# One step of a hybrid decoder on one core: first weights split a quarter ahead, S5 begun two steps later

## The chip, the core and the metric

The kernel runs on one core of one Trainium2 chip. Its five engines work through queues of their own, in order: PE multiplies matrices, DVE (VectorE) and ACT (ScalarE) do elementwise work, POOL (GpSimd) does a little of it and issues most of the transfers between memory and the core's own buffers, SP issues the loads of the weights. An instruction that waits holds up everything behind it on its engine. The metric is the device time of one execution in microseconds (us).

## The reference

One layer serves 1024 tokens of a prompt and 8 single sample tokens together, 1032 columns in all, with a model width of 2048. All arithmetic is float32.

```
h = rmsnorm(x, g_pre);  proj = h @ w_in            # 2048 -> 10240
q, k, v, za, ub, zb, ga, gb = split(proj)
ya = (retention(q, k, v) * silu(za)) @ w_pa        # 8 heads of 128, chunks of 128
yb = (s5(ub) * silu(zb)) @ w_pb                    # diagonal state space, 64 groups of 16 inputs, 64 states
merged = sigmoid(ga) * ya + sigmoid(gb) * yb
out = x + rmsnorm(merged @ w_out, g_post)
```

The final retention and S5 states are outputs too. The S5 branch builds per group a small Toeplitz matrix from its decay parameters, multiplies it with the inputs ub and carries the state from chunk to chunk.

## The kernel before, in words

**Products.** Each float32 operand is split in a high part `hi` (a cast on ACT) and a low part `lo` (what the cast dropped, a subtraction on DVE), and a product is hi·hi + hi·lo + lo·hi, three matmuls. A weight tile ("quarter") is 128 output rows by 512 inputs: `wtile` loads it on SP into `wraw`, casts it to `whi`, subtracts into `wlo`. There are three buffers of each, a, b and c, used in turn. PE cannot use a quarter's low part before DVE has subtracted it.

**The start.** Input rows are loaded and split while the first two blocks of `ub` (128 rows each) are multiplied. Then `linear` multiplies blocks 2 and 3 of `ub` (`M_UB + 2`, `M_UB + 3`, four quarters each, named (34,0) to (35,3) below: 34 and 35 are their numbers among the blocks of `w_in`). Beside these two blocks the *forms* of the input are built (`build_forms`): sums and differences of input blocks, made on DVE into tiles `fo` and `fx` and written by ACT's queue to the memory tensor `fm_d`. Then come two blocks of v, (16,·) and (17,·). The work beside a product is kept in the queue `bg` of generators; `slot()` advances the first of them by one piece, at the points where the main program calls it.

`wnext` gives `linear` its next quarter. If the list `todo` names quarters, it prepares one more than it hands out, so that the next quarter's split is written ahead of the current quarter's products. If `todo` is empty, it prepares a quarter at the moment of its use.

**The steps.** The rest of the multiplication goes by Strassen-like steps. A step `s` is one pair of output blocks for one half of the input; it has seven products, n = 0 to 6, of 24 pairs of matmuls each (L950), and DVE or ACT takes each result out of PE's accumulators (`evac_st`) into tiles `p1`, `u2`, `u3` and `st`, two buffers of each. Four results of a step are finished blocks. At the first visit of a pair they are written to `pt_d`; at the second visit `result` adds what lies in `pt_d` to the tile with an accumulating transfer (L1024) and, four products later, writes a `v` tile out to `v_d` (L1031). All of these go through POOL's queue.

The first six pairs (two of ub, three of v, one of za) are visited in steps 0 to 5, the "short pass", and again in steps 6 to 11, where they are finished. `B0` is 6. From step 12 on, every pair is at a first visit again, until `C0` = 43, where the second pass begins with forms that are staged from step 41 (`change`, with its first twelve loads on SP).

**S5** runs as generators beside the steps: `s5_params` (small DVE operations on parameters) begins at step `B0 + 1`, `s5_all` at `B0 + 4`. For each of 16 blocks, `s5_mats` loads `bc` (L616) and then fills part of the memory tensor `t_d` with zeros: a memset of the tile `zz` on POOL (L619) and a transfer of it, 128 x 4 rows of 112 numbers (L620). There is one `zz` buffer, at a place in the tile `a15` that the ub rows used before, so the memset of one block waits until the transfer of the block before has landed. `zz` shows as `a` in the profile. DVE's first operation on a block reads `bc` (L624).

**What sets the order.** A scheduler places the instructions of each engine. It keeps data dependencies and waits, but it may place an instruction without open dependencies ahead of where the program wrote it. So the 16 zero-fills, which depend only on each other and on `a15`, do not stand one to a block on POOL's queue: they follow each other from the moment on which `a15` is free.

Of the kernel before, what the change touches and what calls it, by code (L numbers as in the profile page):

```python
# [79 lines left out]
def emit(ctx, tc, I, O):  # L80
# [91 lines left out]
    def slot():  # L172
        with ExitStack() as after:
            for ins in anchor.values():
                after.enter_context(tc.issue_after(ins))
            while bg:
                try:
                    next(bg[0])
                    return
                except StopIteration:  # L180
                    bg.popleft()

    def drain():
        while bg:
            slot()
# [6 lines left out]
    def wquarter(wd, m, kq):  # L192
        return wtile(wd[m, :, 4 * kq:4 * kq + 4, :])
# [17 lines left out]
    def wtile(src):  # L211
        turn[0] += 1
        n = turn[0] % (3 + len(more))
        if "pool" in raw_of:
            raw = raw_of["pool"].tile([128, 4, 128], F32, name="wr")
        else:
            raw = more[n] if n < len(more) else wp.tile([128, 4, 128], F32, name="wraw")
        anchor["s"] = nc.sync.dma_start(raw if len(src.shape) == 3 else raw.rearrange("p a b -> p (a b)"), src).ins
        hi, lo = wpair()
        anchor["a"] = A.copy(hi, raw).ins  # L220
        anchor["v"] = sub(lo, raw, hi.bitcast(F32)).ins
        return hi, lo

    def three(ps, w, i, x, t0, t1, first, last):
        wh, wl = w
        xh, xl = x
        T.matmul(ps, wh[:, i, :], xh[:, t0:t1], start=first, stop=False)
        T.matmul(ps, wh[:, i, :], xl[:, t0:t1], start=False, stop=False)
        anchor["p"] = T.matmul(ps, wl[:, i, :], xh[:, t0:t1], start=False, stop=last).ins
# [10 lines left out]
    todo, ahead = deque(), {}  # L240
# [14 lines left out]
    def linear(wd, m, kt, x, evac, thirds=(0, 1, 2), tick=None):  # L255
        ps = {}
        nq = kt // 4
        for kq in range(nq):
            w = wnext(wd, m, kq)
            for t in thirds:  # L260
                t0, t1 = THIRDS[t]
                if kq == 0:
                    ps[t] = mmbank()
                for i in range(4):
                    k = 4 * kq + i
                    three(ps[t][:, 0:t1 - t0], w, i, x(k), t0, t1, k == 0, k == kt - 1)
                if kq == nq - 1:
                    evac(t, ps[t][:, 0:t1 - t0])
                if tick is not None:
                    tick(kq, t)  # L270
            slot()
# [53 lines left out]
    def x_of(k):  # L325
        return xs[k][:, 0, :], xs[k][:, 1, :]
# [15 lines left out]
    def evac_ub(j):  # L342
        def f(t, ps):
            u = ub_new(j) if t == 0 else ubp[j]
            t0, t1 = THIRDS[t]
            w = min(t1, SEQ) - t0
            mul(perm(u, t0 // 8, w // 8), cs(ps[:, 0:w]), cs(rstd[:, t0:t0 + w]))
            if t == 2:
                mul(u[:, 0, 0:8], ps[:, w:w + 8], rstd[:, SEQ:TOK])
                mul(u[:, 7, 136:144], ps[:, w:w + 8], rstd[:, SEQ:TOK])  # L350
                P.dma_start(ub_d[j * 128:(j + 1) * 128], u)
        return f
# [17 lines left out]
    w_in = I["w_in"]  # L370
    M_UB, M_ZB, M_GA, M_GB = 32, 40, 48, 64
# [7 lines left out]
    with tc.tile_pool(name="start", bufs=3) as sp:  # L379
        banks = [[mmbank() for _ in range(3)], [mmbank(), mmbank(), misc()]]  # L380
        w = None
        sqs = deque()
        for k in range(KD):
# [3 lines left out]
            for n, (a, b) in enumerate(parts):  # L387
                nc.sync.dma_start(xr[:, a:b], I["xT"][k, :, a:b])
                if k % 4 == 0 and n == 0:
                    w = [wquarter(w_in, M_UB, k // 4)]  # L390
# [55 lines left out]
    def first_rms():  # L446
        yield
        yield from rms_bcast(ssq, rstd, rm, 1)
# [3 lines left out]
    next(forms_a)  # L452
    bg.append(first_rms())
    bg.append(forms_a)
    for j in (2, 3):
        linear(w_in, M_UB + j, KD, x_of, evac_ub(j), tick=lambda kq, t: slot())

# [351 lines left out]
    def s5_out():  # L809
        A.dma_start(O["s5p"], s5p["fin"])  # L810
        yield
# [4 lines left out]
    def evac_v(h):  # L816
        def f(t, ps):
            t0, t1 = THIRDS[t]
            s = st_tile()[:, 0:t1 - t0]
            mul(s, ps, rstd[:, t0:t1])  # L820
            A.dma_start(v_d[h, :, t0:t1], s)
        return f
# [5 lines left out]
    def popen(name, side, bufs):  # L828
        st = ExitStack()
        return st, st.enter_context(tc.tile_pool(name=name, bufs=bufs, side=side))  # L830
# [10 lines left out]
    B0, C0, N2 = NA, NA + NP, 2 * NP  # L841
# [70 lines left out]
    def prep(g):  # L912
        s, n = divmod(g, 7)
        if g >= lim[0]:
            return
        r = raws

        def sm(name, a, b):
            r[s, name] = wp.tile([128, 4, 128], F32, name="wraw")
            add(r[s, name], r[s, a], r[s, b])  # L920

        if n == 1:
            sm("s1", "21", "22")
            sm("s2", "s1", "11")
        elif n == 3:
            sm("s3", "11", "21")
        elif n == 6:
            sm("s4", "12", "s2")
        f = r[s, ("11", "s2", "12", "s3", "s1", "22", "s4")[n]]
        hi, lo = wpair(qtile_of(steps[s][0], n, 0))  # L930
        anchor["a"] = A.copy(hi, f).ins  # L931
        anchor["v"] = sub(lo, f, hi.bitcast(F32)).ins
        wforms[g] = hi, lo
# [344 lines left out]
    for part_ in range(2):  # L1278
        for j in range(2):
            for kq in (2 * part_, 2 * part_ + 1):  # L1280
                w = wquarter(w_in, 16 + j, kq)
                if part_ and j and kq == 3:
                    prep(0)
                for t, (t0, t1) in enumerate(THIRDS[0:3]):
                    for i in range(4):
                        k = 4 * kq + i
                        three(ps2[j][t][:, 0:t1 - t0], w, i, x_of(k), t0, t1, k == 0, k == KD - 1)
                    if kq == 3:
                        evac_v(j)(t, ps2[j][t][:, 0:t1 - t0])
                slot()  # L1290
# [57 lines left out]
    def stg_open(bufs):  # L1348
        opened["n"] = bufs
        opened["stg"], opened["stgp"] = popen("stg3", "left", bufs)  # L1350
# [43 lines left out]
    for s in range(N2):  # L1394
        kh, p = steps[s]
        if s == 1:
            drain()
            gstack.close()
            fstack, fb2 = popen("fb2", "left", 1)
            bg.append(build_forms(1, fb2, 4, 4, 2))  # L1400
        if s == B0 - 2:
            drain()
            fstack.close()
            gstack, stg = popen("stg1", "left", 12)
        if s == B0 + 1:
            drain()
            gstack.close()
            qstack, s5q = popen("s5q", "left", 1)
            tstack, s5t = popen("s5t", "left", 1)
            bg.append(s5_params())  # L1410
        if s == B0 + 4:
            drain()
            tstack.close()
            tstack, s5w = popen("s5w", "left", 1)
            bg.append(s5_all())
            bg.append(s5_out())
        if s == C0 - 2:
            drain()
            tstack.close()
            qstack.close()  # L1420
            gstack, stg = popen("stg2", "left", 12)
        if s == C0 + 1:
            gstack.close()
            kstack, k2p["pool"] = popen("k2p", "left", 1)
            k2p["bufs"] = 6
            bg.append(order_y())
            cur["cs"] = act.tile([128, 2, TOK], F32, name="a12")
            A.dma_start(cur["cs"][:, 0], I["cos"])
            A.dma_start(cur["cs"][:, 1], I["sin"])
        if s == C0 + 12:  # L1430
            drain()
            kstack.close()
            rstack, rp = popen("ret", "left", 1)
            bg.append(retention())
            kstack, k2p["pool"] = popen("k2q", "left", 1)
            k2p["bufs"] = 3
        if s == N2 - 2:
            while "done" not in K:
                slot()
            rstack.close()  # L1440
            stg_open(8)
        if s == N2 - 1:
            drain()
            kstack.close()
            zstack, zzp = popen("zz", "right", 4)
        for n in range(7):
            g = 7 * s + n
            if n == 1:
                fetch(s + 1)
            prep(g + 2)  # L1450
            evac_st(g, product(g))
            change(g, B0 - 2, 0)
            change(g, C0 - 2, 1)
            transition(g, N2 - 2, "glu", nc.sync)
            late_work(g)
            if s == C0 + 16 and n == 5:
                kstack.close()
                kstack, k2p["oo"] = popen("oo", "right", 1)
            slot()
# [461 lines left out]
```

## Time and profile before

| what | value |
|---|---|
| median of 3 runs | 2549.42 us (2543.85 to 2551.03) |
| the profiled execution | 2547.51 us, span of its instructions 2545.7 us |
| PE busy | 2502.6 us, 98% of the span |
| DVE busy | 2011.6 us, 79% |
| ACT, POOL busy | 997.5 us, 783.0 us |
| chain that ended last | PE 75%, DVE 5%, issue 4%, DMA 2% |

A timeline row gives an instruction's start and duration in us, engine, line, what it writes and reads, and in brackets how long its engine stood idle before it and what ended that. Line L85 is a helper through which all two-operand DVE operations go, so there the tile names tell what is done. A windows row gives the busy time of each engine in a stretch, then the granted PE clock as a share of full speed, the busy share of the DMA engines and what they moved. PE is busy nearly always; what a change can win or lose shows in the few places where PE stands idle or runs at a lower clock.

### The profile page before, as it was taken

To read this page: it belongs to the slowest core of one execution; us is meant where nothing else is said; L and a number is where in the kernel's file an instruction comes from. 1 tells how busy PE (TensorE), PEld (TensorE's weight loads), DVE (VectorE), ACT (ScalarE), POOL (GpSimd) and SP (SyncE) were. 2 spreads that over 40 slices of the span, in tenths; PEclk is the share of its full clock that TensorE was granted. 3 is DMA by queue.
4 is the path that set the end of the run, shared out by engine and by line. 5 is a ranking of instruction groups with operands and counts; after the bars stand their busy time and mean duration, and the time that the engine had idled before them with its cause. 6 is when DMAs were issued, how large, how long until landed. Compare 5 with 4: busy or idle time off the path is not lost.

```text
span 2545.7 us, 52887 instructions
## 1 busy us (share of the span) xinstructions
PE 2502.6 (98%) x20026; PEld 2454.4 (96%) x20026; DVE 2011.6 (79%) x4212; ACT 997.5 (39%) x1787; POOL 783.0 (31%) x1308
## 2 busy tenths in 40 slices
PE   9899999999999999999999999999999999999998
PEld 8899999999999999999999999999999999999976
DVE  7567897988988987667986676667897788989885
ACT  7042532333333332353334434444552432445532
POOL 0021235222223222123335444443332222433320
PEclk9999999999999999999999999999999999999999
DMA  7769666444344344488889988887888689857784
GB/s 243 237 212 307 191 172 194 128 136 132 121 133 131 125 131 158 154 224 210 213 218 262 240 222 221 216 231 223 290 280 291 213 244 311 297 198 176 210 302 140
DMA packets 238559, 530.77 MB, mean 208 GB/s; under 512 B 34928, under 2 KB 62016, under 8 KB 237536
## 3 DMA queue, kind: packets, MB, share of 16 engines
q0 software_dynamic: 106080, 310.20, 42.8%
q1 hardware_dynamic: 93280, 162.47, 20.3%
q10 hardware_dynamic: 38944, 54.71, 6.7%
q8 instruction: 158, 2.59, 0.4%
q14 instruction: 97, 0.79, 0.1%
HBM read 351.88 MB, written 175.37 MB: 207 GB/s over the span
## 4 chain that ended last, share of the span: by engine, by line
PE 75%; DVE 5%; issue 4%; DMA 2%; POOL 1%; ACT 0%; DVEq 0%; POOLq 0%; ACTq 0%
PE acc L950 65%; PE acc L1819 5%; DVE u L85 1%; DVE a L85 1%; PE misc L780 1%; PE misc L779 1%; PE misc L1175 1%; PE misc L1185 1%; PE misc L1154 1%; PE misc L730 1%; DMA t_d<-a 0%; PE misc L1187 0%; DVE wlob L85 0%; DMA a<-mg_d 0%; DMA stg<-fo_d 0%
## 5 line engine op out<-in xcount | busy, mean ns | idle before, releaser
L950 PE MATMUL acc<-a,whib 128*128 128x256 f32 (+1 forms) x3816 | 631.2, 284 | 7.0 <-DVE u L85 5.9
L950 PE MATMUL acc<-a,whic 128*128 128x256 f32 (+1 forms) x3808 | 629.9, 284 | 7.1 <-DVE u L85 5.6
L950 PE MATMUL acc<-a,whia 128*128 128x256 f32 (+1 forms) x3800 | 627.1, 284 | 0.8 <-ACT whia L931 0.5
L950 PEld LDWEIGHTS acc<-a,whib 128*128 128x128 f32 x3816 | 527.5, 189 | 9.8 <-DVE u L85 5.4
L950 PEld LDWEIGHTS acc<-a,whic 128*128 128x128 f32 x3808 | 525.9, 188 | 10.4 <-DVE u L85 3.5
L950 PEld LDWEIGHTS acc<-a,whia 128*128 128x128 f32 x3800 | 523.6, 188 | 5.6 <-issue 3.0
L950 PE MATMUL acc<-a,wlob 128*128 128x256 f32 (+1 forms) x1908 | 397.5, 283 | 0.0
L950 PE MATMUL acc<-a,wloc 128*128 128x256 f32 (+1 forms) x1904 | 396.9, 283 | 0.4 <-DVE wloc L85 0.4
L950 PE MATMUL acc<-a,wloa 128*128 128x256 f32 (+1 forms) x1900 | 395.1, 282 | 0.0
L950 PEld LDWEIGHTS acc<-a,wloc 128*128 128x128 f32 x1904 | 298.2, 188 | 1.4 <-DVE wloc L85 1.4
L950 PEld LDWEIGHTS acc<-a,wlob 128*128 128x128 f32 x1908 | 298.9, 188 | 0.3
L950 PEld LDWEIGHTS acc<-a,wloa 128*128 128x128 f32 x1900 | 297.0, 188 | 0.3 <-DVE wloa L85 0.2
L931 ACT CAST whic<-wraw 128x512 fp32r<-128x512 f32 x148 | 92.0, 622 | 239.6 <-PE acc L950 178.5
L931 ACT CAST whia<-wraw 128x512 fp32r<-128x512 f32 x146 | 90.7, 621 | 230.2 <-PE acc L950 163.3
L931 ACT CAST whib<-wraw 128x512 fp32r<-128x512 f32 x146 | 90.8, 622 | 230.0 <-PE acc L950 166.4
L85 DVE TENSOR_TENSOR wraw<-wr 128x512 f32<-128x512 f32 x220 | 151.0, 687 | 2.9 <-DVE mhalf L1101 0.4
L85 DVE TENSOR_TENSOR wloa<-wraw,whia 128x512 fp32r<-128x512 f32 x154 | 105.6, 686 | 55.1 <-ACT whia L931 37.3
L85 DVE TENSOR_TENSOR wloc<-wraw,whic 128x512 fp32r<-128x512 f32 x156 | 107.0, 686 | 50.8 <-ACT whic L931 36.7
L931 ACT CAST whib<-wr 128x512 fp32r<-128x512 f32 x111 | 68.9, 621 | 196.3 <-PE acc L950 161.7
L85 DVE TENSOR_TENSOR a<-stg,a 128x516 fp32r<-128x516 f32 (+1 forms) x224 | 136.1, 639 | 10.2 <-ACT a L274 5.7
L931 ACT CAST whia<-wr 128x512 fp32r<-128x512 f32 x110 | 68.3, 621 | 190.6 <-PE acc L950 168.7
L931 ACT CAST whic<-wr 128x512 fp32r<-128x512 f32 x109 | 67.7, 621 | 186.1 <-PE acc L950 154.3
(458 smaller groups left out, 4255.1 us busy)
## 6 DMA issues: line engine op xcount, KB each, us to landing
wr<-in_w_in SPq DMA_DIRECT2D x296, 256.0 KB
pt_d<-u POOLq DMA_DIRECT2D x74, 258.0 KB, 3.3
u<-pt_d POOLq DMA_DIRECT2D x74, 258.0 KB, 5.0
wr<-in_w_out SPq DMA_DIRECT2D x64, 256.0 KB
wr<-in_w_outB SPq DMA_DIRECT2D x64, 256.0 KB
stg<-fm_d POOLq DMA_DIRECT2D x60, 258.0 KB, 4.7
pt_d<-st POOLq DMA_DIRECT2D x37, 258.0 KB, 3.7
pt_d<-p POOLq DMA_DIRECT2D x37, 258.0 KB, 3.0
```

Source lines behind the costliest of these rows:

```text
L85: return (eng or V).tensor_tensor(out, a, b, op)
L730: T.matmul(ps[:, q * 144:(q + 1) * 144], W1[:, g, :], U[:, g, :], start=True, stop=True)
L779: T.matmul(o, Tm[:, g, :], U[:, g, 0:136], start=True, stop=False)
L780: T.matmul(o, W3[:, g, 1:9, :], X[:, g, 0:136], start=False, stop=True)
L931: anchor["a"] = A.copy(hi, f).ins
L950: anchor["p"] = T.matmul(o, a[:, i, :], x, start=first and i == 0 and a is wh and b is xh, stop=n in (2, 5, 6) and i == 3 and a is wl, ski ...
L1154: T.matmul(ps[:, c * 128:(c + 1) * 128], kt[:, 4 * i + c, :], vt[:, 4 * i + c, :], start=True, stop=True)
L1175: T.matmul(ps[:, c * 128:(c + 1) * 128], kT[:, cs], qT[:, cs], start=True, stop=True)
L1185: T.matmul(o, S[:, n], vt[:, n], start=True, stop=n == 0)
L1819: anchor["p"] = T.matmul(ps[c], a, b, start=k == 0 and a is xh and b is wh, stop=k == KD - 1 and a is xl).ins
```

## The change

Two edits, both of order; nothing is computed differently.

```diff
     bg.append(first_rms())
     bg.append(forms_a)
+    todo.extend((w_in, m, kq) for m in (M_UB + 2, M_UB + 3) for kq in range(4))
+    todo.append((w_in, 16, 0))
     for j in (2, 3):
         linear(w_in, M_UB + j, KD, x_of, evac_ub(j), tick=lambda kq, t: slot())
...
-                w = wquarter(w_in, 16 + j, kq)
+                w = ahead.pop((16 + j, kq), None) or wquarter(w_in, 16 + j, kq)
...
         if s == B0 + 1:
             drain()
             gstack.close()
+        if s == B0 + 3:
             qstack, s5q = popen("s5q", "left", 1)
             tstack, s5t = popen("s5t", "left", 1)
             bg.append(s5_params())
-        if s == B0 + 4:
+        if s == B0 + 6:
             drain()
             tstack.close()
             tstack, s5w = popen("s5w", "left", 1)
```

The first edit names the eight quarters of ub blocks 2 and 3, and the first quarter of v, in `todo`, so that each is split one quarter ahead. The second moves the start of `s5_params` from step 7 to step 9, and that of `s5_all` from step 10 to step 12. Lines from 455 on stand two lower in the changed file, from 1408 on three lower.

**DVE, blocks 2 and 3 of ub, where the forms are made.** Before: `wloc_952` is the low part of quarter (35,1), `wloa_1011` that of (35,2), `wlob_1053` that of (35,3); `fx_624` and `fx_626` are the third pair of input blocks whose forms are made.

```order
L428 SCALAR_TENSOR_TENSOR fx_626<-fx_626,g_pre_107,rstd_104 128x1032
L85 TENSOR_TENSOR fo_934<-fx_624 128x516
L85 TENSOR_TENSOR fo_936<-fx_624,fx_626 128x516
L85 TENSOR_TENSOR fo_938<-fx_626,fo_934 128x516
L85 TENSOR_TENSOR wloc_952<-wraw_949,whic_951 128x512
L85 TENSOR_TENSOR fo_940<-fx_626,fo_938 128x516
L428 SCALAR_TENSOR_TENSOR fx_898<-fx_898,g_pre_107,rstd_104 128x1032
L428 SCALAR_TENSOR_TENSOR fx_900<-fx_900,g_pre_107,rstd_104 128x1032
L85 TENSOR_TENSOR fo_993<-fx_898 128x516
L85 TENSOR_TENSOR fo_995<-fx_898,fx_900 128x516
L85 TENSOR_TENSOR fo_997<-fx_900,fo_993 128x516
L85 TENSOR_TENSOR wloa_1011<-wraw_1008,whia_1010 128x512
```

In the changed kernel `wloc_888` is the low part of (35,1) and `wloa_958` that of (35,2):

```order
L85 TENSOR_TENSOR fo_872<-fx_620,fx_622 128x516
L85 TENSOR_TENSOR fo_874<-fx_622,fo_870 128x516
L85 TENSOR_TENSOR wloc_888<-wraw_885,whic_887 128x512
L85 TENSOR_TENSOR fo_876<-fx_622,fo_874 128x516
L85 TENSOR_TENSOR ubp_604<-ubp_604,rstd_104 128x128x8
L85 TENSOR_TENSOR ubp_604<-ubp_604,rstd_104 128x8 x2
L428 SCALAR_TENSOR_TENSOR fx_624<-fx_624,g_pre_107,rstd_104 128x1032
L428 SCALAR_TENSOR_TENSOR fx_626<-fx_626,g_pre_107,rstd_104 128x1032
L85 TENSOR_TENSOR fo_940<-fx_624 128x516
L85 TENSOR_TENSOR fo_942<-fx_624,fx_626 128x516
L85 TENSOR_TENSOR fo_944<-fx_626,fo_940 128x516
L85 TENSOR_TENSOR wloa_958<-wraw_955,whia_957 128x512
```

Each low part moved forward by one group of forms: (35,1) stands ahead of the third pair's forms, at the place behind the second pair's third `fo`; (35,2) stands where (35,1) stood; and the low part of (35,3) takes the place behind the fourth pair's third `fo`, where (35,2) stood.

**POOL, from the last write of ub rows on (step 9).** Before, two zero-fills (`a15`) stand ahead of the load of `bc` for S5's first block:

```order
L1009 DMA ub_d_84<-a14_3784 128x1152
L619 MEMSET a15_4470 128x112
L1031 DMA v_d_88<-st_4249 128x516
L620 DMA t_d_85<-a15_4470 128x4x112
L1024 DMA u3_4294<-pt_d_101 128x516
L619 MEMSET a15_4470 128x112
L620 DMA t_d_85<-a15_4470 128x4x112
L616 DMA bc_4468<-in_bc 128x256
L1024 DMA p1_4150<-pt_d_101 128x516
```

In the changed kernel the zero-fills begin at the same place, behind the same write of ub rows, but the load of `bc` has moved back by two steps; these are its neighbours (`u3_4766` and `st_4723` are results of step 11):

```order
L621 MEMSET a15_4938 128x112
L622 DMA t_d_85<-a15_4938 128x4x112
L1026 DMA st_4723<-pt_d_101 128x516
L621 MEMSET a15_4938 128x112
L622 DMA t_d_85<-a15_4938 128x4x112
L1033 DMA v_d_88<-st_4723 128x516
L621 MEMSET a15_4938 128x112
L622 DMA t_d_85<-a15_4938 128x4x112
L1026 DMA u3_4766<-pt_d_101 128x516
L618 DMA bc_4936<-in_bc 128x256
```

Between the write of ub rows and `bc` stand thirteen zero-fills now, where two stood, and among them all accumulating transfers and stores of steps 9 and 10 and two of step 11.

**DVE, where it first reads `bc`.** Before, in the order of its queue:

```order
L85 TENSOR_TENSOR u2_4202<-acc_4318,u2_4202 128x516
L85 TENSOR_TENSOR wlob_4438<-wr_4169,whib_4437 128x512
L624 TENSOR_SCALAR a15_4470<-bc_4468,sgn_3499 128x64
L85 TENSOR_TENSOR B1_4474<-cr_3743,bc_4468 128x64
L85 TENSOR_TENSOR a15_4470<-ci_3744,a15_4470 128x64
```

And in the changed kernel:

```order
L85 TENSOR_TENSOR u2_4681<-acc_4786,u2_4681 128x516
L85 TENSOR_TENSOR wloa_4906<-wr_4648,whia_4905 128x512
L626 TENSOR_SCALAR a15_4938<-bc_4936,sgn_3989 128x64
L85 TENSOR_TENSOR B1_4942<-cr_4241,bc_4936 128x64
L85 TENSOR_TENSOR a15_4938<-ci_4242,a15_4938 128x64
```

The neighbours are the same (`u2` is the last result of a step), two steps later: step 9's `u2` before, step 11's now.

## The prediction

> **What bounds the kernel now.** I began with the page. PE is busy for all but 43 us of the span, so an edit of order can win or lose only where PE stands still.
>
> ```profile
> span 2545.7 us, 52887 instructions
> PE 2502.6 (98%) x20026; PEld 2454.4 (96%) x20026; DVE 2011.6 (79%) x4212; ACT 997.5 (39%) x1787; POOL 783.0 (31%) x1308
> ```
>
> The list of PE's waits names the places. The largest is one wait for a low part of a weight; the next, summed over nine waits, is for results that DVE takes out of PE's accumulators.
>
> ```profile
> PE acc L950 <- DVE u L85: 11.7, 9, 3.6
> PE mm L229 <- DVE wloc L85: 9.2, 1, 9.2
> ```
>
> *The first place* is quarter (35,1). Its high part was cast long before. On DVE the subtraction stands behind forms that wait until earlier forms have been written to memory:
>
> ```profile
> 85.06 1.97 DVE L85 TENSOR_TENSOR ubp<-ubp,rstd 128x1024 f32<-128x1024 f32 x1
> ...
> 93.53 1.30 DVE L85 TENSOR_TENSOR fo<-fx 128x516 f32<-128x516 f32 x2 [3.34 <-DMA fm_d<-fo]
> ...
> 95.36 0.69 DVE L85 TENSOR_TENSOR wloc<-wraw,whic 128x512 fp32r<-128x512 f32 x1
> ...
> 104.42 0.68 DVE L85 TENSOR_TENSOR wloa<-wraw,whia 128x512 fp32r<-128x512 f32 x1
> ```
>
> The casts of (35,1), (35,2) and (35,3), in that order, show that ACT is not what is late:
>
> ```profile
> 74.64 0.62 ACT L220 CAST whic<-wraw 128x512 fp32r<-128x512 f32 x1 [7.26 <-PE mm L228]
> 80.52 0.62 ACT L220 CAST whia<-wraw 128x512 fp32r<-128x512 f32 x1 [5.26 <-DVE ubp L85]
> 86.54 0.62 ACT L220 CAST whib<-wraw 128x512 fp32r<-128x512 f32 x1 [5.40 <-PE mm L229]
> ```
>
> On PE, these rows are the start of (35,1), its wait, the wait of (35,2), the start of (35,3) and that of the quarter after it; the windows row shows the clock after the wait.
>
> ```profile
> 85.82 0.34 PE L227 MATMUL mm<-a,whic 128*128 128x384 f32 x1
> ...
> 96.10 0.69 PE L229 MATMUL mm<-a,wloc 128*128 128x384 f32 x1 [9.17 <-DVE wloc L85]
> ...
> 105.16 0.44 PE L229 MATMUL mm<-a,wloa 128*128 128x384 f32 x1 [1.35 <-DVE wloa L85]
> ...
> 110.56 0.34 PE L227 MATMUL mm<-a,whib 128*128 128x384 f32 x1
> ...
> 116.21 0.34 PE L227 MATMUL mm<-a,whic 128*128 128x384 f32 x1
> ```
>
> ```profile
> 96.00:100.00 4.00, 3.90 (x12) 3.90 (x13) 3.15 (x4) 0.00 (x0) 0.00 (x0) 0.50 1.03 406
> ```
>
> An undisturbed quarter takes 116.21 - 110.56 = 5.65 us. Three took 116.21 - 85.82 = 30.4 instead of 16.95, so 13.4 us were lost: 9.17 and 1.35 of waiting, and the rest, 2.9, while PE ran at half its clock after the wait.
>
> *The second place* is the start of S5. PE stalls twice on an evacuation (the first and third row); the others are the starts of following products.
>
> ```profile
> 374.96 1.23 PE L950 MATMUL acc<-a,whic 128*128 128x256 f32 x4 [3.28 <-DVE u L85]
> ...
> 379.20 0.64 PE L950 MATMUL acc<-a,whia 128*128 128x256 f32 x4
> ```
>
> ```profile
> 422.08 1.16 PE L950 MATMUL acc<-a,whib 128*128 128x256 f32 x4 [3.60 <-DVE u L85]
> ...
> 426.58 0.64 PE L950 MATMUL acc<-a,whic 128*128 128x256 f32 x4
> ...
> 429.40 0.64 PE L950 MATMUL acc<-a,whia 128*128 128x256 f32 x4
> ```
>
> A product takes 429.40 - 426.58 = 2.82 us, a step of seven 19.7. The products behind the stalls took 4.24 and 4.50, so 1.4 and 1.7 more. The two stalls cost 3.28 + 1.4 = 4.7 and 3.60 + 1.7 = 5.3 us, together 10.0. What is behind them stands in DVE's rows:
>
> ```profile
> 364.02 0.68 DVE L85 TENSOR_TENSOR wlob<-wr,whib 128x512 fp32r<-128x512 f32 x1
> 369.20 0.32 DVE L624 TENSOR_SCALAR a<-bc,sgn 128x64 f32<-128x64 f32 x1 [4.50 <-DMA bc<-in_bc]
> ...
> 374.22 0.68 DVE L85 TENSOR_TENSOR u<-p,acc 128x516 f32<-128x516 f32 x1
> ...
> 412.87 1.10 DVE L85 TENSOR_TENSOR ksb<-AR,B 128x512 f32<-128x512 f32 x1 [5.68 <-DMA t_d<-ksb]
> ```
>
> Both times DVE waits for a transfer that POOL issued late, `bc` and then the store of `ksb`, and the evacuation stands behind. POOL's rows tell why it is late:
>
> ```profile
> 365.10 0.19 POOL L619 MEMSET a<- 128x112 f32 x1 [1.43 <-DMA t_d<-a]
> 365.61 0.78 POOL L620 DMA_DIRECT2D t_d<-a  x1 [0.31 <-POOL a L619]
> 366.37 0.56 POOL L616 DMA_DIRECT2D bc<-in_bc  x1
> 366.90 0.95 POOL L1024 DMA_DIRECT2D p<-pt_d  x1
> ...
> 379.27 0.20 POOL L619 MEMSET a<- 128x112 f32 x1 [1.91 <-DMA t_d<-a]
> 379.77 0.75 POOL L620 DMA_DIRECT2D t_d<-a  x1 [0.30 <-POOL a L619]
> ...
> 382.30 0.19 POOL L619 MEMSET a<- 128x112 f32 x1 [0.26 <-DMA t_d<-a]
> ...
> 387.71 0.19 POOL L619 MEMSET a<- 128x112 f32 x1 [1.99 <-DMA t_d<-a]
> ...
> 405.95 0.19 POOL L619 MEMSET a<- 128x112 f32 x1 [2.71 <-DMA t_d<-a]
> ```
>
> Each memset of a zero-fill waits for the transfer before it, and the accumulating loads and stores of the v blocks queue up behind.
>
> **The first edit, term by term.** It adds no instruction; it moves four subtractions of 0.69 us on DVE, and loads on SP. The low part of (35,1) now stands where DVE was at 85.06, so it is ready by 85.8, and (35,1) runs from 85.8 to 91.5 without a wait. (35,2) does 0.7 us of high-part matmuls and waits from 92.2 for its low part, which has the old place of (35,1) and ends at 95.36 + 0.69 = 96.05. The 1.97 us of ub scaling that now follow the moved split push nothing: DVE stood idle for 3.34 us at 93.53. So PE waits 3.9 us, pays 1.4 for the clock as at 374.96, and ends (35,2) at 96.05 + 4.95 + 1.4 = 102.4. (35,3) works 0.35 us, waits for the place of the row at 104.42, until 105.1, and ends at 105.1 + 5.3 = 110.4. That is 5.8 us before 116.21. Two of the moved weight loads, 256 KB each, now fall among the writes that the forms wait for; at the 406 GB/s of the window each takes 0.65 us there, and part of that falls on the path. I take a gain of **5.0**. Bounds: 0, if forms and low parts get later by as much as they moved, and 13.4, if no wait were left. A loss is not among them, since DVE's idle time covers 0.69 us per split. Behind the place PE runs nearly without a stop until step 9, so the gain stays; DVE's forms keep their end, as they wait for transfers.
>
> **The second edit, term by term.** It adds and removes no instruction either. `s5_params`, all of S5's DVE, ACT and PE work, and POOL's loads of `bc`, U, X, `x0` and the `ksb` stores move back two steps, 39.4 us. Not so the zero-fills: on POOL they begin behind the same write of ub rows as before. So POOL has eleven more of them ahead of `bc`. With P for the time from one zero-fill's memset to the next, `bc` is issued 11 P + 0.95 us after its place of before (0.95 for one accumulating load more, the row at 366.90), while DVE comes to it 39.4 us later. The lateness grows by 11 P + 0.95 - 39.4.
>
> For P the trace has: 3.03 us, the shortest (379.27 to 382.30); 4.56, the mean of four between 387.71 and 405.95, with v traffic among them as it will be; 5.1, the mean of the eight from 365.10 to 405.95, which have S5's own loads among them too; and 3.9 from the median landing of 3.4 plus 0.5 from memset to issue.
>
> ```profile
> t_d<-a POOLq DMA_DIRECT2D x13, 224.0 KB, 3.4
> ```
>
> In the changed kernel S5's loads are gone from between, so I take 4.4, just under the nearest row. Then `bc` is later by 48.4 + 0.95 - 39.4 = 10.0 us, DVE's wait grows from 4.5 to 14.5, and PE's stall at the fourth product of step 12 from 3.28 to 13.3. Behind DVE's waiting instruction stand the rest of that block's first operations, a split, a weight sum and the evacuation `u`, the same as now (369.20 to 374.22). With 2.9 for the clock, as after the wait of 9.17, the new stall costs **16.2**. It takes the place of the old first one (4.7). The old second one (5.3) goes: by the time DVE reaches the next `ksb`, POOL has had the stall to work off its queue, and only three zero-fills are left. The edit costs 16.2 - 10.0 = 6.2.
>
> The end of S5 comes two steps nearer to the staging of the second pass. SP's loads for it could start here, and ACT first read them here:
>
> ```profile
> 1007.77 0.80 SPq L889 DMA_DIRECT2D stg<-fm_d  x2
> ```
>
> ```profile
> 1061.73 0.63 ACT L274 CAST a<-stg 128x516 fp32r<-128x516 f32 x1
> ```
>
> Moved by 39.4, the loads start at 1047.2, 14.5 us ahead of that read. I cost this at nothing; without that cover each further microsecond would be one of PE's, and SP's weight loads stand behind these transfers.
>
> **The sum.** -5.0 + 6.2 = +1.2 us: 2547.51 + 1.2 = 2548.7 for the profiled execution. The median of the runs is 1.9 above that execution, so I forecast **2550 us**: no change, which here means within 0.3% (7.6 us), about what a measurement of this kernel can tell.
>
> **Rivals.**
>
> *Short zero-fills: faster.* If P is near the shortest row, 3.03, then 11 P + 0.95 = 34.3 is less than 39.4, `bc` is in time, and both old stalls go: -10.0 - 5.0 = -15.0, 2534 us. The change is faster than 0.3% as soon as the new stall costs less than 7.4 in all, which is P below about 3.75. For it: with `bc`, U, X and `ksb` gone from between, POOL's queue and the transfers are freer. Against it: the four periods in the stretch most like the coming one average 4.56. The Trainium skill, page "DMA: Bandwidth & Descriptors", section "Anatomy of one DMA — SWDGE (gpsimd) path", fits a transfer from this queue as about 2.0 us plus its bytes over 436 GB/s; for 224 KB that is an estimate of 2.5 us, so P near 3.0 and this rival's time. The trace agrees in its shortest case (379.77 to 382.30, 2.53 us) and not in its median of 3.4.
>
> *Long zero-fills: slower.* At P = 5.1 the lateness grows by 17.7, the stall is 20.9 + 2.9 = 23.8, and the whole is +8.8, 2558 us. It decides from P = 5.0 on. For it: that was the mean over the eight periods, and accumulating loads and stores of three steps now crowd between zero-fills without a pause. Against it: those eight held loads of S5 that have left. The Trainium skill, same page, section "Specifications", wants pieces of at least 512 bytes for full rate; a zero-fill's rows are 448 bytes. No row here separates that from waiting in the queue.
>
> *The first edit gives nothing,* because the writes of forms bound the stretch (DMA share 1.03 in the window) and PE only waits elsewhere: +6.2, 2555.6, still no change.
>
> *The change does not move the stall at all,* since the zero-fills, which make POOL late, are not moved: then DVE waits about as before, -5.0, 2544, no change.
>
> **How the numbers follow.** Forecast 0.42, first edit void 0.07, stall as before 0.06: same 0.55. Short zero-fills 0.28: faster. Long ones 0.17: slower. The range runs from the rival at 2534 to just past the one at 2558: 2534 to 2560. The likeliest case alone, with P from 3.9 to 4.8, spans 2544 to 2556.
>
> **What would show it.** Right: PE has no wait of 9 us near 86, but two of 2 to 4 near 92 and 103, and the v quarters start about 5 us earlier; DVE's wait for `bc` near step 12 is 10 us or more, with one PE stall of as much; thirteen memsets lie between the last ub write and `bc` on POOL; no `ksb` wait of DVE afterwards. Wrong: `bc` in time, or a PE stall on stage loads near 1060. The forecast falls if P is outside 3.75 to 5.0.

## The result, and the profile after

| | median | range | runs |
|---|---|---|---|
| kernel before | 2549.72 us | 2543.85 to 2554.17 | 20 |
| changed kernel | 2546.10 us | 2541.58 to 2550.60 | 20 |

The ratio is 0.9985, with a 95% interval of 0.9978 to 0.9992: 3.6 us faster by the medians, 2.0 to 5.6 by the interval. That is inside the 0.3% which I called no change, and inside my range of 2534 to 2560. But with twenty runs each it is clear of nothing, and it goes the other way than the +1.2 that I had forecast. The sum came out about 5 us too high.

The profiled execution of the changed kernel took 2549.9 us, near the upper end of its runs, and that of before (2547.51) lies in the lower half of its own. So these two profiles stand +2.4 apart where the medians stand -3.6 apart. They are compared place by place below, never by their spans.

```profile
span 2548.1 us, 52901 instructions
PE 2503.8 (98%) x20026; PEld 2456.2 (96%) x20026; DVE 2010.5 (79%) x4212; ACT 996.7 (39%) x1787; POOL 781.2 (31%) x1308
```

The list of PE's waits (total, number, longest) still has the same two kinds on top, but the longest of each is now at a new place:

```profile
PE acc L952 <- DVE u L85: 15.9, 8, 10.6
PE mm L229 <- DVE wloa L85: 8.1, 1, 8.1
```

*The first place*, in the timeline of the changed kernel (DVE's and PE's rows; start, duration, instruction, idle time before it):

```profile
87.24 0.34 PE L227 MATMUL mm<-a,whic 128*128 128x384 f32 x1
...
96.91 0.70 DVE L85 TENSOR_TENSOR fo<-fx 128x516 f32<-128x516 f32 x1 [4.00 <-DMA fm_d<-fo]
...
101.11 0.68 DVE L85 TENSOR_TENSOR wloa<-wraw,whia 128x512 fp32r<-128x512 f32 x1
...
101.85 0.69 PE L229 MATMUL mm<-a,wloa 128*128 128x384 f32 x1 [8.10 <-DVE wloa L85]
...
114.30 0.34 PE L227 MATMUL mm<-a,whic 128*128 128x384 f32 x1
```

Quarter (35,1) no longer waits. (35,2) waits 8.1 us for a low part that I had expected ready at 96.05 and that was ready at 101.8; (35,3) then does not wait at all. The three quarters took 114.30 - 87.24 = 27.06, that is 10.1 more than three undisturbed ones (16.95); before it was 13.4. In this pair of profiles the first edit gained 3.3 us at its place.

*The second place* is the start of S5. POOL's, DVE's and PE's rows:

```profile
352.39 0.19 POOL L621 MEMSET a<- 128x112 f32 x1 [0.48 <-DMA ub_d<-a]
358.88 0.19 POOL L621 MEMSET a<- 128x112 f32 x1
...
406.46 0.19 POOL L621 MEMSET a<- 128x112 f32 x1
408.26 0.92 POOL L618 DMA_DIRECT2D bc<-in_bc  x1
...
413.23 0.26 DVE L626 TENSOR_SCALAR a<-bc,sgn 128x64 f32<-128x64 f32 x1 [11.90 <-DMA bc<-in_bc]
...
418.88 1.23 PE L952 MATMUL acc<-a,whib 128*128 128x256 f32 x4 [10.62 <-DVE u L85]
...
423.76 0.64 PE L952 MATMUL acc<-a,whic 128*128 128x256 f32 x4
```

The mechanism is the forecast one: thirteen memsets stand ahead of `bc`, DVE waits for `bc`, PE for the evacuation behind it. The sizes are smaller: P is (406.46 - 358.88) / 11 = 4.33 (4.4 forecast), DVE's wait 11.9 (14.5), PE's stall 10.6 (13.3). The product behind the stall took 423.76 - 418.88 = 4.88 instead of 2.82, so 2.1 for the clock (2.9). The windows rows show it (PE clock is the column before the last two):

```profile
416.00:420.00 4.00, 1.12 (x5) 1.12 (x6) 4.00 (x7) 0.00 (x0) 2.31 (x5) 0.50 0.83 211
...
424.00:428.00 4.00, 4.00 (x37) 4.00 (x36) 3.86 (x15) 1.01 (x2) 1.18 (x3) 1.00 0.75 241
```

The Trainium skill, page "TensorE: Matmul & The Clock Gate", section "Part 1: The HAM clock gate", says that an idle array falls to half rate and comes back after about 3.4 us of work; that is an estimate of 1.7 us per stall. The 2.1 here is a little more: the granted clock stayed at 0.50 for about 4.3 us of work, from 418.88 to near 423.2.

*What the start of S5 costs as a whole* is read from ACT's copy of the first product of each step. In the kernel before, an undisturbed step takes 285.41 - 265.64 = 19.77 us. These are the copies of steps 5, 6 and 9 to 13:

```profile
265.64 0.58 ACT L1063 COPY p<-acc 128x516 f32<-128x516 f32 x1
285.41 0.58 ACT L1063 COPY p<-acc 128x516 f32<-128x516 f32 x1
...
345.47 0.58 ACT L1063 COPY p<-acc 128x516 f32<-128x516 f32 x1
366.36 0.58 ACT L1063 COPY p<-acc 128x516 f32<-128x516 f32 x1
390.99 0.59 ACT L1063 COPY p<-acc 128x516 f32<-128x516 f32 x1
412.94 0.59 ACT L1063 COPY p<-acc 128x516 f32<-128x516 f32 x1
438.84 0.58 ACT L1063 COPY p<-acc 128x516 f32<-128x516 f32 x1
```

And in the changed kernel those of steps 9, 12 and 13:

```profile
342.48 0.59 ACT L1065 COPY p<-acc 128x516 f32<-128x516 f32 x1
...
402.95 0.59 ACT L1065 COPY p<-acc 128x516 f32<-128x516 f32 x1
435.55 0.59 ACT L1065 COPY p<-acc 128x516 f32<-128x516 f32 x1
```

I call a step's time less 19.77 its loss. Step 12 of the changed kernel lost 435.55 - 402.95 - 19.77 = 12.8. Before, steps 7 to 12 lost 15.1 in all, 4.9 of it in step 10 and 6.1 in step 12. In the changed kernel steps 7 to 14 lost 16.6. After that both show the same losses step for step, only two steps apart. So in these two profiles the second edit cost 1.5; other profiles of the same two orders, further down, differ by several us.

The second pass's stage loads now start at 1046.04 and are first read at 1060.96, without a wait: that cover held, as costed.

```profile
1046.04 6.68 SPq L891 DMA_DIRECT2D stg<-fm_d  x10
...
1060.96 0.63 ACT L274 CAST a<-stg 128x516 fp32r<-128x516 f32 x1
```

### The profile page after: what moved, and what is told of

It is laid out like the page before. It is cut to its first block, busy times and chain, and to the rows that moved or that the text cites. A ratio compares the mean times of both kernels' runs of the same rounds, so it can differ in the third digit from the quotient of the medians.

```text
span 2548.1 us, 52901 instructions
## 1 busy us (share of the span) xinstructions
PE 2503.8 (98%) x20026; PEld 2456.2 (96%) x20026; DVE 2010.5 (79%) x4212; ACT 996.7 (39%) x1787; POOL 781.2 (31%) x1308
## 4 chain that ended last, share of the span: by engine, by line
PE 81%; issue 6%; DMA 6%; DVE 4%; POOL 3%; ACT 0%; POOLq 0%; DVEq 0%; ACTq 0%; SPq 0%
PE acc L952 67%; PE acc L1822 3%; PE mm L229 1%; PE mm L227 1%; PE mm L228 1%; DMA t_d<-a 1%; DMA fm_d<-fo 1%; DVE a L85 1%; DMA a<-in_xT 1%; PE misc L782 1%; PE misc L781 1%; DVE u L85 1%; PE misc L1177 1%; PE misc L1187 1%; PE misc L1156 1%
## 5 line engine op out<-in xcount | busy, mean ns | idle before, releaser
L952 PEld LDWEIGHTS acc<-a,whib 128*128 128x128 f32 x3816 | 528.1, 189 | 18.2 <-DVE u L85 11.8
```

The source lines that it names most:

```text
L952: anchor["p"] = T.matmul(o, a[:, i, :], x, start=first and i == 0 and a is wh and b is xh, stop=n in (2, 5, 6) and i == 3 and a is wl, ski ...
```

## The experiments

**Theory after the result:** both edits act where I put them, but the second was priced some 5 us too high; and what makes `bc` late is its place behind the zero-fills on POOL. **Rivals:** the first edit gives more than 5 and the second costs what I said; or `bc` is late because the DMA engines are full, wherever it is issued. All differences in time below are against runs of the kernel before on the same chip; the code is shown as a change of the changed kernel, unless the text names another.

### Each edit alone

```diff
-        if s == B0 + 3:
         ...
-        if s == B0 + 6:
+        if s == B0 + 4:
```

> The kernel before with the first edit alone (quarters named in todo). By the prediction's sum: -5.0, so 2544.7 against a kernel before of 2549.7. By the two traces (the first step begins 1.9 us earlier although the changed run was 1.4 late before the place): -3.3, 2546.4. In both, PE waits once or twice near 92 to 103 and not near 86, and S5's two old stalls stay (3.3 and 3.6 of waiting). Rival, the edit gives nothing because the writes of the forms bound the stretch: 2549.7.

Measured: 2545.52 against 2550.86 (ratio 0.9978, 0.9967 to 0.9990), -5.3 by the medians, -2.6 to -8.4 by the interval. PE's waits at the place (list of waits of this kernel):

```profile
PE mm L229 <- DVE wloa L85: 5.0, 1, 5.0
PE mm L229 <- DVE wlob L85: 1.6, 1, 1.6
```

The same two waits as I forecast (3.9 and 2.4), in the same order. This profile is the mildest of the eight with one quarter ahead: (35,2) waits 5.0 to 8.9 in them, (35,3) at most 1.6. The rival (the writes bound the stretch, no gain) falls. The second edit alone:

```diff
-    todo.extend((w_in, m, kq) for m in (M_UB + 2, M_UB + 3) for kq in range(4))
-    todo.append((w_in, 16, 0))
...
-                w = ahead.pop((16 + j, kq), None) or wquarter(w_in, 16 + j, kq)
+                w = wquarter(w_in, 16 + j, kq)
```

> The kernel before with the second edit alone (S5 two steps later). By the prediction's sum: +6.2, 2555.9. By the two traces, where the new stall is 10.6 of waiting and about 12.7 in all, and steps 7 to 10 lose 0.7 less: +1.5, 2551.2. By the medians of the whole change (-3.6), if the first edit is worth the forecast 5.0: +1.4. Rival, the second edit is worth nothing or gains: 2549.7 or less, which the changed kernel's medians would allow if the first edit is worth only 3.3.

Measured: 2551.95 against 2550.86 (1.0004, 0.9996 to 1.0013), +1.1 by the medians, -1.0 to +3.3 by the interval. The +6.2 of the prediction is outside. DVE's and PE's rows of this kernel:

```profile
413.15 0.26 DVE L624 TENSOR_SCALAR a<-bc,sgn 128x64 f32<-128x64 f32 x1 [8.80 <-DMA bc<-in_bc]
...
418.93 1.23 PE L950 MATMUL acc<-a,whib 128*128 128x256 f32 x4 [7.59 <-DVE u L85]
```

On POOL the same thirteen zero-fills stand ahead of `bc` as in the changed kernel, and the wait is 8.8 where it was 11.9 there. With one profile of each, this alone does not tell scatter from the absence of the first edit; a third profile with this order, below, has 6.6. -5.3 and +1.1 add to -4.2; the whole change gave -3.6.

### Taking away what makes the zero-fills wait for each other

All sixteen blocks write the same zeros, so one memset is enough. In the changed kernel:

```diff
-        P.memset(zz, 0.0)
+        if b == 0:
+            P.memset(zz, 0.0)
```

> The changed kernel with the memset of zz only for the first block: the same zeros are written, but no zero-fill has to wait until the one before it has landed. If the chain memset, transfer, landing on POOL's queue makes bc late: DVE's wait of 11.9 for bc and PE's stall of 10.6 go, some 12.7 us: 2546.1 - 12.7 = 2533.4. Rival, bc is late because the transfers themselves and the accumulating loads fill the DMA engines: bc's wait stays at 8 or more, 2546. Second rival: the thirteen transfers, now let loose together, hold up the weights' loads or the write of ub rows; then a new stall stands near 350 to 360.

Measured: 2542.38 (0.9963, 0.9952 to 0.9975), -8.5 by the medians where the changed kernel has -3.6, and the two intervals do not overlap. POOL's and DVE's rows:

```profile
352.52 0.19 POOL L622 MEMSET a<- 128x112 f32 x1 [1.50 <-DMA ub_d<-a]
...
402.81 0.56 POOL L1034 DMA_DIRECT2D v_d<-st  x1 [6.52 <-DMA st<-pt_d]
...
403.92 0.90 POOL L618 DMA_DIRECT2D bc<-in_bc  x1
...
408.16 0.25 DVE L627 TENSOR_SCALAR a<-bc,sgn 128x64 f32<-128x64 f32 x1 [7.12 <-DMA bc<-in_bc]
```

Less than half of what I expected. `bc` is still the last of a row of thirteen zero-fills: they no longer wait for one another, but accumulating loads and v stores stand between them, and those stores wait (6.52 us in the row at 402.81). In the kernel before, with S5 at its old place:

> The kernel before with the memset of zz only for the first block, S5 at its old place. If the chain of zero-fills was behind both old stalls (bc near 369, the store of ksb near 412): both go, 10.0 us, 2539.7, and what the second edit did is then no more than to trade these two for one. If the thirteen transfers still stand ahead of the ksb store on the queue and only the bc wait goes: about -5, 2545. Rival, contention and not the chain: 2549.7.

Measured: 2549.24 against 2550.86 (0.9993, 0.9984 to 1.0001), nothing that can be told from no change. DVE's list of waits around S5's start:

```profile
DVE a L625 <- DMA bc<-in_bc: 3.9, 1, 3.9
DVE ksb L85 <- DMA t_d<-ksb: 3.0, 1, 3.0
```

Both waits stay, shorter than in the kernel before (4.5 and 5.7) but about as long as with the first edit alone (3.5 and 4.6). By the times, the chain of memsets is a part of the cause in the changed kernel, not all of it; at the old place no part can be told.

### Moving only `bc`

The changed kernel, with the first block's `bc` on SP's queue and every zero-fill left where it is:

```diff
-        P.dma_start(bc, I["bc"][:, g0:g0 + 4, :])
+        (P if b else nc.sync).dma_start(bc, I["bc"][:, g0:g0 + 4, :])
```

> The changed kernel with one transfer moved: the first block's load of bc goes through SP's queue, not POOL's; the thirteen zero-fills stay as they are. If the place of bc behind the zero-fills on POOL is the cause of the stall at step 12: DVE's wait for bc (11.9) and PE's stall of 10.6 go and no ksb wait takes their place, since POOL is through with the zero-fills by 409 and DVE stores ksb only some 30 us later. Step 12 loses 0 to 1 instead of 12.8; some 12 us less than the changed kernel, about 2534 where that has 2546. Rival, what DVE needs next (U, X, or the ksb store, all still behind the zero-fills on POOL) is as late as bc was: then a wait of 5 or more stands on the next of them and the gain is under half.

Measured: **2534.15** against 2548.72 (0.9940, 0.9926 to 0.9953), -14.6. Step 12 lost 0.4. SP's and DVE's rows:

```profile
399.89 0.19 DVE L85 TENSOR_TENSOR phi<-phi,u 128x32 f32<-128x32 f32 x1
...
400.11 0.59 SPq L618 DMA_DIRECT2D bc<-in_bc  x1
...
403.60 0.25 DVE L626 TENSOR_SCALAR a<-bc,sgn 128x64 f32<-128x64 f32 x1 [1.11 <-DMA bc<-in_bc]
```

From issue to use `bc` took 3.5 us, so the DMA engines were not too full for it, and the rival falls. The stall is the place of `bc` on POOL; nothing else that S5 needs is late. The rows show one thing more: even on SP's queue `bc` is issued only at 400.11, right behind the last operation of `s5_params`. The next two experiments follow that up.

### When `bc` may be loaded at all

The changed kernel with only `s5_params` back at step 7:

```diff
-        if s == B0 + 3:
             qstack, s5q = popen("s5q", "left", 1)
```

> The changed kernel with s5_params back at step 7 and only s5_all two steps later. It tests the assumption that the zero-fills begin where they did. If the small operations of s5_params on DVE hold up the ub rows: POOL's first memset is 2.2 us later again against the copy of step 9 (12.1 behind it, not 9.9), bc's wait and PE's stall grow by as much over the changed kernel's 11.9 and 10.6, to about 14 and 13, steps 7 to 9 lose 1.9 to 2.7 and steps 10 and 11 less than 1.1; in all 2 to 3 us above the changed kernel, 2548.5. Rival, the earlier start in the changed kernel is scatter: memset near 10 behind the copy, stalls as in the changed kernel, 2546.

Measured: **2535.77** against 2548.72 (0.9950, 0.9937 to 0.9962), -13.0: 13 us below what I expected, and the wrong way. POOL's and DVE's rows:

```profile
354.25 0.19 POOL L621 MEMSET a<- 128x112 f32 x1 [1.79 <-DMA ub_d<-a]
...
361.33 0.19 POOL L621 MEMSET a<- 128x112 f32 x1 [0.93 <-DMA t_d<-a]
...
362.60 0.56 POOL L618 DMA_DIRECT2D bc<-in_bc  x1
...
400.74 0.25 DVE L626 TENSOR_SCALAR a<-bc,sgn 128x64 f32<-128x64 f32 x1
```

What I meant to test stays undecided: the first memset is 12.2 behind the copy of step 9 (342.09), not 9.9 as in the changed kernel, and steps 7 to 9 lost 2.1. But with `s5_params` at step 9 that distance is 9.8 in the second edit alone, 11.8 with one memset and 12.0 with `bc` over SP, so the 9.9 can be scatter, which was the rival. And `bc` now stands behind two zero-fills again, although `s5_all` begins at step 12 as in the changed kernel. The scheduler places `bc` as soon as nothing it depends on is open, and what it depends on is not the step but its buffer: the tiles of S5 take the memory in which those of `s5_params` lay. The changed kernel with a buffer of its own for `bc`:

```diff
+        if name == "bc":
+            return s5q.tile(shape, F32, name=name)
         if name not in FIXED:
             return s5w.tile(shape, F32, name=name, bufs=bufs)
```

> The changed kernel with the buffer of bc taken from the memory that is kept for all of S5 instead of that in which the tiles of s5_params lie before; all transfers stay on their queues. If bc is issued late because its buffer is free only when s5_params is through, and by then stands behind thirteen zero-fills: bc now stands behind four of them, is in time, no stall is left at step 12, and the time is that of the kernels that load bc over SP or run s5_params early: about 12 below the changed kernel, 2534. Rival, with bc out of the way U and X, still late, hold DVE: a stall of 5 or more stays at step 12, 2540 or more.

Measured: 2537.19 against 2549.10 (0.9949, 0.9937 to 0.9962), -11.9. The view of the tile `bc` (duration, then first and last start) and POOL's row of `U`:

```profile
L620 POOL DMA_DIRECT2D bc<-in_bc x16: 542/549/557, 292.7 to 938.9; - x16
```

```profile
408.56 1.14 POOL L704 DMA_DIRECT2D U<-ub_d  x1
```

With the memory freed, `bc` is issued at 292.7, ahead of all zero-fills where I had expected it behind four, and step 12 lost 0.2. Step 9 lost 3.8; there DVE waited for the load of `s5_params`, twice as long as in the changed kernel (2.63), and no run shows why:

```profile
344.49 0.21 DVE L483 TENSOR_SCALAR e_t<-prm 128x96 f32<-128x96 f32 x1 [5.31 <-DMA prm<-in_prm]
```

`U` is as late as `bc` was, and nothing waits for it. The mechanism is shown twice: `bc` is late because its buffer is free only when `s5_params` ends, and because thirteen zero-fills have by then been queued ahead. In the changed kernel's profile `s5_params` ends here:

```profile
398.73 0.19 DVE L85 TENSOR_TENSOR phi<-phi,u 128x32 f32<-128x32 f32 x1
```

By then ten of the thirteen memsets had run. The last three zero-fills, and the loads and stores among them, held `bc` for the other 9.3 us, to 408.26.

### S5 one step later still

```diff
-        if s == B0 + 3:
+        if s == B0 + 4:
...
-        if s == B0 + 6:
+        if s == B0 + 7:
```

> The changed kernel with S5 one more step later (s5_params from step 10, s5_all from step 13). If thirteen zero-fills ahead of bc are all that makes it late: DVE comes to bc 19.7 us later, when POOL has worked them off, so bc is in time, no stall of over 1 us stands at steps 12 to 14, and the gain over the changed kernel is about 12, less what the loads of the second pass's first tiles now cost: they started at 1046.0 and the first is read at 1061.0, so 19.7 later they are up to 8 late: 2534 to 2542. Rival, the lateness comes with S5's own loads wherever they stand: a stall of some 10 at step 13, 2546 or more.

Measured: 2541.12 against 2548.72 (0.9971, 0.9961 to 0.9981), -7.6. POOL's and DVE's rows:

```profile
422.69 0.54 POOL L618 DMA_DIRECT2D bc<-in_bc  x1
...
427.20 0.25 DVE L626 TENSOR_SCALAR a<-bc,sgn 128x64 f32<-128x64 f32 x1 [6.91 <-DMA bc<-in_bc]
```

The stall moved to step 13 and stayed (8.6 lost), which is the rival; I had not yet seen that `bc` is tied to `s5_params`, and that moved too. All sixteen zero-fills now stand ahead of `bc`. The time is at the upper edge of what I said, and not from the cause I gave.

### What the second edit is worth without the late `bc`

The first edit alone (S5 at its old place), with `bc` over SP:

> The first edit alone (S5 at its old place), with the first block's bc loaded over SP. It prices the second edit once bc is out of the way: the changed kernel with the same load over SP has 2534. If the old ksb stall (4.6 of DVE waiting, 4.2 lost at its step) is the zero-fills' work as the prediction says: the bc wait goes and the ksb wait stays, 2545.3 - 3 to 4 = 2541.5, so that the second edit is worth some -7 with bc over SP where it costs about 1 without. Rival, the ksb wait goes too, because DVE is earlier: then both have about 2535 and the second edit is worth nothing in either form.

Measured: 2546.54 against 2549.10 (0.9989, 0.9980 to 0.9998), -2.6: not better than the first edit without it. SP's and DVE's rows:

```profile
359.10 0.33 SPq L618 DMA_DIRECT2D bc<-in_bc  x1
...
409.73 1.02 DVE L85 TENSOR_TENSOR ksb<-AR,B 128x512 f32<-128x512 f32 x1 [10.25 <-DMA t_d<-ksb]
```

Step 10 lost 0.4 instead of 4.1, and step 12 lost 13.3 instead of 4.2: DVE came to the `ksb` store earlier and waited there instead. In this run a stall removed at `bc` came back behind it, at the `ksb` stores that POOL issued late. At the new place it does not (2534.15). So with `bc` out of the way the second edit is worth 12 us, where the prediction made it a loss.

### Two quarters ahead

```diff
-        if todo:
+        while todo and len(ahead) < 3:
             fetch_w()
```

> The changed kernel with the quarters split two ahead instead of one. If what is left of the loss at the first place (10.1 us in the changed kernel's profile, 8.6 with the first edit alone) is only the low part of (35,2) standing behind the third pair's forms: its split now stands where that of (35,1) stood, PE does not wait for it, and waits at most 3 for that of (35,3): 4 to 7 us less than the changed kernel, about 2541. Rival, ACT's casts, which now wait for buffers that PE still reads, hold up the writes of the forms behind them on ACT's queue, or the writes fill the DMA engines anyway: the wait of PE moves to (35,3) and stays near 8, 2546.

Measured: 2544.12 against 2548.72 (0.9978, 0.9969 to 0.9987), -4.6 where the changed kernel has -3.6: less than I expected, and the two intervals overlap. PE's and ACT's rows:

```profile
108.14 0.62 ACT L220 CAST whic<-wraw 128x512 fp32r<-128x512 f32 x1 [18.99 <-DMA fm_d<-fo]
...
108.81 0.69 PE L227 MATMUL mm<-a,whic 128*128 128x384 f32 x1 [5.28 <-ACT whic L220]
```

No low part is waited for at this place any more. Instead PE waits 5.3 us for the high part of the first quarter of v: its cast stands on ACT's queue behind the writes of the forms. That is the rival turned round: not the casts hold up the writes, but the writes, which wait for DVE's forms, hold up a cast. What is removed on DVE's queue comes back, smaller, on ACT's.

At S5 this kernel has thirteen zero-fills ahead of `bc` like the changed one. DVE's and PE's rows there:

```profile
405.88 0.25 DVE L626 TENSOR_SCALAR a<-bc,sgn 128x64 f32<-128x64 f32 x1 [6.58 <-DMA bc<-in_bc]
...
411.63 1.23 PE L952 MATMUL acc<-a,whib 128*128 128x256 f32 x4 [5.39 <-DVE u L85]
```

So the three profiles with this order have waits of 11.9, 8.8 and 6.6 for `bc`, and 12.8, 9.7 and 7.1 lost in step 12. Two ahead joined with the two cures of the second place:

> The changed kernel with bc over SP and with two quarters ahead. If the two places are independent: the gains add, -12 and -2 against the changed kernel, 2532. Rival, the gain of two ahead was a lucky set of runs: 2534.

> The changed kernel with s5_params back at step 7 and two quarters ahead. Same mechanism as bc over SP, by another way (bc stands behind two zero-fills again, DVE comes to it 40 us later): 2533, within 2 of the kernel with bc over SP and two ahead. Rival: the small operations of s5_params in steps 7 to 9, which cost 2 there, make it 2 to 3 slower than that one.

Measured: 2534.59 (0.9939, 0.9925 to 0.9953) and 2534.19 (0.9943, 0.9931 to 0.9956) against 2549.10. Neither can be told from `bc` over SP alone (2534.15), nor from each other. All three lie 11 to 12 us below the changed kernel, the fastest here. That two ahead adds 2 us to the whole is not shown by the times. The traces show it at its place: in the three profiles with two ahead the first step's copy stands at 159.8 to 160.9, in the eight with one ahead at 161.1 to 164.1.

## Why the prediction was right or wrong

Losses at S5's start, each from the copies of steps as above (up to the step from which all profiles agree):

| kernel | steps counted | loss | largest step |
|---|---|---|---|
| before | 7 to 12 | 15.1 | step 12, 6.1 |
| first edit alone | 7 to 12 | 13.3 | step 12, 4.2 |
| first edit, `bc` over SP | 7 to 12 | 18.1 | step 12, 13.3 |
| changed | 7 to 14 | 16.6 | step 12, 12.8 |
| second edit alone | 7 to 14 | 13.4 | step 12, 9.7 |
| changed, two quarters ahead | 7 to 14 | 11.8 | step 12, 7.1 |
| changed, one memset | 7 to 14 | 13.2 | step 12, 8.1 |
| changed, `bc` in its own place | 7 to 14 | 7.7 | step 9, 3.8 |
| changed, `bc` over SP | 7 to 14 | 5.0 | step 13, 2.2 |
| changed, `s5_params` early | 7 to 14 | 4.7 | step 13, 2.2 |

**The first edit: right in place and about in size.** -5.0 forecast, -5.3 alone (-2.6 to -8.4); that the two agree so closely is more than that interval can show. By the profiles it is a little less: in eight with one quarter ahead the first step's copy stands at 162.4 on average (161.1 to 164.1), in the three without the edit at 166.2 (165.6 to 166.6), 3.7 apart. One working step was off. I gave the low part of (35,2) the old time of (35,1), ready at 96.05; it was ready at 97.7 to 101.8 in these eight profiles, since the forms ahead of it came later too. So the sign I had named, two waits of 2 to 4, did not come: it is one of 5.0 to 8.9, then one of 1.6 at most. Part of what that cost was won back at (35,3), whose forecast wait was 2.4.

**The second edit: the step that failed.** "The new stall costs 16.2", against which the old ones (10.0) were set for a net +6.2. Measured alone it is +1.1 (-1.0 to +3.3); in the three profiles with the new stall step 12 lost 12.8, 9.7 and 7.1 in place of the 16.2. The old stalls, steps 10 and 12, lost 11.0 before and 8.3 with the first edit alone. So what the edit put in and what it took away are about equal, and the sign of the rest is not shown. Where the 16.2 was mis-sized can be read in the rows of the changed kernel. Counted from the copy of step 9, `bc` was issued at 366.37 - 345.47 = 20.9 before and at 408.26 - 342.48 = 65.8 now, later by 44.9 and not by 11 P + 0.95 = 49.4. Of these 4.5 us:

- 2.2: the first memset came 9.9 behind that copy, not 12.1. I had written that the zero-fills begin "behind the same write of ub rows as before". They do; this write was issued 0.8 earlier, and POOL was through with waiting for it 1.4 sooner. Why stays open: with `s5_params` at step 9 the distance is 9.8 to 12.6 in the profiles.
- 1.0: the first period, 6.5 instead of 7.5.
- 0.8: P, 4.33 instead of 4.4.
- 0.4: the rest, between the last memset and `bc`.

DVE came to `bc` 39.6 later, as forecast (39.4), and the transfer itself took 5.0 from issue to use instead of 2.8, which gave 2.1 back. So the wait grew by 44.9 + 2.1 - 39.6 = 7.4, from 4.5 to 11.9. The clock behind the stall, 2.9 forecast, was 2.1. The other two profiles with this order shift the shares: P is 4.11 in the second edit alone and 3.96 with two quarters ahead, which is 3.2 and 4.9 of their 6.9 and 7.7 us, while the first memset's share is 2.3 and 0.5. So P was forecast too long in all three, by 0.8 to 4.9 us over the eleven periods, and the first period by 1.0 to 1.9. Moving `s5_params` I had costed at nothing; steps 7 to 9 lost 1.9 before, and the steps 9 to 11 in which it now runs 1.2, a difference that the other profiles do not bear out (up to 3.8 in steps 9 to 11).

**Right:** thirteen memsets ahead of `bc`; one wait in the place of two; no wait for `ksb` afterwards; no stall on the stage loads; P inside 3.75 to 5.0. My case against short zero-fills held: P was 3.96 to 4.33. The Trainium skill, page "DMA: Bandwidth & Descriptors", section "Anatomy of one DMA — SWDGE (gpsimd) path", had led to an estimate of P near 3.0; the means of these traces lie above it. **Only half right:** that POOL is late because each memset waits for the transfer before it. Without these waits the whole gained 4.9 us more, and a stall of 5.9 stayed, no shorter than the 5.4 of the mildest profile that has the waits. What puts `bc` behind the zero-fills is the memory of its buffer, which I had not looked at. The prediction didn't need it for the time, since the order showed `bc` there; it would have needed it to say that the same edit, with `bc` free, gains 12 to 15 us.

**Open:** why the waits of one and the same order differ by several us between profiles (6.6 to 11.9 for `bc`, 5.0 to 8.9 for the low part of (35,2)). With one profile of each kernel a term of 3 us cannot be checked; the timed runs of single edits, and several profiles that share an order, can.

## What to carry to other kernels

When a stage is moved, ask not only what is queued ahead of its first load but from when that load may be issued: a buffer laid over the tiles of an earlier stage ties the load to that stage's end. A load that is small and first needed is worth a place of its own in memory, or another queue; here either gave 8 to 12 us that moving the stage alone did not. And before a wait of one profile is put into a sum or explained to a tenth, look how much the same wait differs among profiles that share its order.

## What was not expected of the hardware

After a stall of 10.6 us PE ran at half its clock for about 4.3 us of its own work and lost 2.1; after the 9.2 us before, it ran at half its clock for about 5.2 us and lost 2.7 (the other 0.3 of the 2.9 fell to the quarter with the wait of 1.35); after the waits of 3.28 and 3.60 it lost 1.4 and 1.7. The longest stall did not cost the most clock. And taking the waits out of POOL's row of zero-fills bought little: `bc` was then issued 51.4 us after the first memset (352.52 to 403.92), although no zero-fill waited for another; with the waits it was 55.9, 53.5 and 51.0 in the three profiles of that order.
